# Hybrid state-space and delta-rule layer: the remaining adaLN vectors computed behind the mixers instead of beside them

## The chip, the core and the metric

One core of a Trainium2 chip runs the whole layer as one program. The metric is the device time of one execution in microseconds (us), a median over several runs. The engines have these names below: PE is TensorE (matrix products; PEld are its weight loads), DVE is VectorE, ACT is ScalarE, POOL is GpSimd, SP is the queue that issues most DMAs. Each engine works through its own instructions strictly in the order in which the program lists them; semaphores make it wait for others. SBUF is the on-chip memory, PSUM holds the results of matrix products, DRAM is the memory outside.

## The reference

512 tokens of width 2048 pass through one layer, in float32:

```python
mod = (silu(c) @ w_ada + b_ada)                       # 6 vectors of 2048: adaLN
sh_m, sc_m, g_m, sh_f, sc_f, g_f = split(mod, 6)
h = layer_norm(x) * (1 + sc_m) + sh_m
u, q, k, v, z, beta, a, gate_s, gate_g = split(h @ w_in)
y_s = s5_mixer(u, ...) @ w_up_ssm                     # state-space mixer, 64 groups
y_g = gated_deltanet(q, k, v, z, beta, a, ...) @ w_up_gdn   # delta rule, 8 heads, 8 chunks of 64 tokens
m = sigmoid(gate_s) * y_s + sigmoid(gate_g) * y_g
x = layer_norm(alpha * x + g_m * (m @ w_mix_out), ln1)
h = layer_norm(x) * (1 + sc_f) + sh_f
x = layer_norm(alpha * x + g_f * swiglu(h), ln2)
```

The two vectors `sh_m` and `sc_m` are needed before anything else. The other four (`g_m`, `sh_f`, `sc_f`, `g_f`) are a product of one row of 2048 with a 2048 x 8192 part of `w_ada`, 67.1 MB of float32, and they are what the change moves. `g_m` is first needed in the output projection `m @ w_mix_out`, `sh_f` and `sc_f` in the layer norm behind it, `g_f` in the feed-forward part.

## The kernel before

**The main line** is a sequence of large matrix products. Every weight block (128 x 1024 values) is loaded by SP into `raw`, cast by ACT to `whi` (the part that fits float32r) and subtracted by DVE into `wlo` (the rest); a product is then three PE passes, two with `whi` and one with `wlo`. There are three buffers each of `raw`, `whi` and `wlo`; a block is split two blocks ahead of its use and loaded three ahead of its split. A block feeds 24 PE passes of 512 columns, but 12 in the output projection, where only 256 of the tokens are in work at a time.

**The stages** are, in order: the start (layer norm, `sh_m`, `sc_m`, the first input columns); the mixer stage, where the products for q, k, v and z of eight delta-rule heads and seven gate pairs form the main line; the remaining gates; the gated unit (GLU) and the two up projections; the output projection in two halves of 256 tokens, each with four quarters of 512 columns; the feed-forward groups; the last layer norm.

**Side lines** are woven into the main line. A side line is a Python generator: `s5_line` (eight batches of the state-space mixer, one after the other, most of it on POOL), `gdn_prep_line` and `gdn_solve_line` (the delta-rule heads), `ln_half` (the two halves of the layer norm behind the output projection), and `ada_rest` (the four remaining adaLN vectors). The class `Order` keeps rough prices of all instructions and, after every three PE passes (`o.tick()`), emits the next piece of those side lines whose inputs it takes to be there. So the order on every engine is settled when the program is built. `o.until(...)` and `o.drain(line)` emit side lines' pieces with no main-line product between them until a condition holds; `o.drain(lnl)` stands behind the output projection and forces all that is left of the first `ln_half` there.

**One adaLN unit** is 512 columns of one vector, and there are 16 units, one after the other. `ada_line` loads 16 slices of 128 x 512 (`w`, 256 KB each, four buffers, on SP's queue) and adds them up, each times a column of `silu(c)`, into `aacc`. While the mixers' memory is in use (the list `P2` is empty) all 16 slices are DVE instructions, and a slice is emitted only when `Order` takes DVE to be nearly idle. Once the mixers' memory has been given back (`P2` is filled by `switch()`), every third slice from the second on (5 of 16) is scaled by ACT instead and added by POOL into a second sum `aacc2`, one DVE addition joins the sums, and DVE's state is no longer asked. Then PE sums over partitions: for `g_m` and `g_f` by one product with a constant (`ada_row_line`, four DVE instructions ahead of it put in the bias; ACT copies the row out and SP stores it to DRAM), for `sh_f` and `sc_f` by four small products (`ada_cols_line`).

In the kernel before, `ada_rest` is added to the side lines when the delta rule's convolution weights are ready, ahead of the first head, so all its units are emitted in the mixer stage. Helpers record every instruction, so the profile's L170 is any instruction of DVE, ACT, POOL or SP, L211 any matrix product and L216 any transpose; tiles tell them apart: `pm` and `px_fo` are the main line's products, `px_gd`, `g_...`, `St`, `vn` and `TTfull` the delta rule's, `px_s` and `s_...`, `s5...` the state-space mixer's, `px_ada` and `aacc` adaLN's.

Of the kernel before, what the change touches and what calls it, by code (L numbers as in the profile page):

```python
# [16 lines left out]
PSUM = bass.MemoryType.PSUM  # L17
DRAM = bass.MemoryType.DRAM
M, A, S = ALU.mult, ALU.add, ALU.subtract
# [17 lines left out]
def shape_constants():  # L37
    """128-wide masks, then masks of 64 x 64 diagonal blocks, stacked twice over the partitions."""
    i = np.arange(128)[:, None]
    j = np.arange(128)[None, :]  # L40
    m = [np.eye(128), j < i, i <= j, i // 16 == j // 16]
    i, j = i % 64, np.arange(64)[None, :]
    pair = (i // 2 == j // 2)
    m += [i == j, -1.0 * (pair & (j < i)), -1.0 * (pair & (i < j))]
    m += [(i // b == j // b + 1) & (i // b % 2 == 1) for b in (2, 4, 8, 16, 32)]
    return np.concatenate([a.astype(np.float32) for a in m], axis=1)
# [10 lines left out]
class Order:  # L57
    """Emission order of all engines: a main line of matrix products with side lines woven in.

    A rough model of the engines tells when each result is there, so that a side line's next piece is emitted  # L60
    about when its inputs are.
    """
    LAT = 0.12
# [12 lines left out]
    def _first(self, ap):  # L76
        """When the slot of a tile that is written for the first time gets free."""
        t = ap.tensor
        nm = ap.name
        if nm in self.ready or not hasattr(t, "tag_meta") or t.tag_meta is None:  # L80
            return 0.0
        q = self.slots.setdefault(t.tag, [])
        q.append(nm)
        n = t.tag_meta.bufs
        return self.last.get(q[-n - 1], 0.0) + self.LAT if len(q) > n else 0.0
# [73 lines left out]
class Engine:  # L159
    """An engine's instructions, with their rough price told to the order."""  # L160

# [110 lines left out]
def s5_setup(k, p, lam_re, lam_im, log_dt):  # L272
    """Powers of the discretised poles and their B factors, in [(re|im, state), group] and [(group parity, state), pair]."""
    nc, v, act, pool, pe = k.nc, k.v, k.act, k.pool, k.pe
# [98 lines left out]
def s5_batch(k, j, prm, d_col):  # L373
    """One tile of 128 channels (8 groups): u^T comes from k.du, 2 * gelu(y)^T goes to k.dz."""
    v, act, pool, pe, ld = k.v, k.act, k.pool, k.pe, k.ld
    b_re, b_im, c_re, c_im = prm
    s, t = k.s5, k.t5
# [106 lines left out]
    for ri in range(2):  # L484
        for rj in range(2):
# [3 lines left out]
            x = St[:, :, ri, 1:8, 0:7]  # L489
# [38 lines left out]
def gdn_setup(k, p, psb, a_log, dt_bias, conv_w, norm_w):  # L528
    """psb rows 0..7: beta logits, rows 8..15: decay logits, over tokens."""
    v, act, pool, pe, ld = k.v, k.act, k.pool, k.pe, k.ld  # L530
# [76 lines left out]
def gdn_conv(k, h, which, ps):  # L607
    """Causal convolution over tokens, out of PSUM."""
    s = k.gd
    a = k.tg("qkv"[which])  # L610
    col = lambda w: s.cw[:, 24 * w + 8 * which + h:24 * w + 8 * which + h + 1]
    k.act.activation(a, ps, AF.Identity, scale=col(3))
    for w in (2, 1, 0):
        d = 3 - w
        k.v.scalar_tensor_tensor(out=a[:, d:512], in0=ps[:, 0:512 - d], scalar=col(w), in1=a[:, d:512], op0=M, op1=A)
    return a
# [21 lines left out]
def gdn_prep(k, h):  # L638
    """All of a head that does not wait for the chunks before: decays, norms, the strictly lower matrix, q k^T."""
    v, act, pool, pe = k.v, k.act, k.pool, k.pe  # L640
    s, t = k.gd, k.tg
    r = Ctx()
# [104 lines left out]
def gdn_solve(k, h, r):  # L747
    """The inverse of the unit lower matrix by doubling blocks, then the chunks' recurrence and the head's output."""
    v, act, pool, pe = k.v, k.act, k.pool, k.pe
# [136 lines left out]
class Weights:  # L886
    """The stream of weight blocks, loaded and split into two float32r parts ahead of their use."""

# [63 lines left out]
    def poll(self):  # L952
        """The next block's load, once its slot is free."""
        i = self.loaded
        if i < len(self.specs) and i < self.cut + NB:
            o = self.k.o
            if i < NB or o.last.get(self.names[i - NB], 0.0) <= o.clock:
                self.load(i + 1)
# [3 lines left out]
def kernel(ctx, tc, x, c, w_ada, b_ada, w_in, lam_re, lam_im, log_dt, b_re, b_im, c_re, c_im,  # L962
# [39 lines left out]

# [1 line left out]
    ws = Weights(k, wpool)  # L1004
# [47 lines left out]

# [1 line left out]
    cst = cpool.tile([128, 128], F32, name="cst")  # L1054
# [18 lines left out]
    def by_pos(a):  # L1073
        """A tile whose tokens are ordered by their position in the chunk first, read in the tokens' order."""
        return a.rearrange("p (s c) -> p c s", s=8)

# [1 line left out]
    def split(hi, lo, src, eng=None):  # L1078
# [8 lines left out]
    def after(first):  # L1087
        """Between products: the next block's split and the side lines."""
        if first:
            ws.run_ahead()  # L1090
        o.tick()
# [11 lines left out]
    def gemm2(kt, acts, done, pre=None):  # L1103
        """Two neighbouring 128-column tiles, K in blocks of 8 slices."""
        pss = [psum_mm(), psum_mm()]
# [17 lines left out]
    def ada_line(p, col0):  # L1123
        """Per-partition partial sums of 512 adaLN columns."""
        acc = p.tile([128, 512], F32, name="aacc", tag="aacc", bufs=1)
# [34 lines left out]
    def ada_cols_line(p, j, q, dst, plus):  # L1160
        """512 columns of adaLN vector j, as columns."""
        acc = yield from ada_line(p, 2048 * j + 512 * q)
# [6 lines left out]
    def ada_row_line(p, j, q):  # L1169
        """Half of 512 columns of adaLN vector j, to a row in DRAM."""  # L1170
        acc = yield from ada_line(p, 2048 * j + 512 * q)
# [10 lines left out]

# [1 line left out]
    hT = []  # L1184
# [158 lines left out]

# [1 line left out]
    adp = ctx.enter_context(pool_of(name="adp", bufs=1, side="right"))  # L1345
# [15 lines left out]

# [1 line left out]
    gps, sps = ExitStack(), ExitStack()  # L1363
# [32 lines left out]
    o.until(lambda: k.cw_ready)  # L1396
    o.add(ada_rest())
    gate_next = iter(range(0, 32, 2))
# [7 lines left out]
    for h in range(8):  # L1406
# [9 lines left out]
        k.heads[h, 3] = z  # L1416
# [1 line left out]
    def switch():  # L1418
        """The mixers' memory becomes the operands' of the later products."""
        o.drain(s5l)  # L1420
# [22 lines left out]
        k.ada_deep = True  # L1443
        o.add(operands())

    def bt(dtype=F32R):
# [17 lines left out]

# [1 line left out]
    k.ada_deep = False  # L1466
# [62 lines left out]
    def row_of(src, q):  # L1529
        """A quarter of a row of 2048, on all partitions."""  # L1530
        return row_to(P2[1].tile([128, 512], F32, name="grow", tag="grow", bufs=1), src, q)
# [4 lines left out]

# [1 line left out]
    xa = [[None] * 4 for _ in range(4)]  # L1538
    h2 = [[None] * 16 for _ in range(2)]

    def ln_stats(st):
        """Mean, rstd and -mean * rstd of a token tile, as columns."""
        mv = cpool.tile([128, 2], F32, name="mv", tag="mv", bufs=4)
# [13 lines left out]
    def affine(r, st, g, b, how):  # L1557
        """((r - mean) * rstd) * g + b, in place; how: 0 on DVE, 1 shared, 2 without DVE."""
        if how == 0:
# [7 lines left out]
    def ln_half(hf, new_big):  # L1567
        """LN1, then LN0 with the FFN's adaLN, for 256 tokens; alpha * x1 stays in xa, h2^T goes to h2[hf]."""
        rows = []
# [84 lines left out]

# [1 line left out]

    def ffn_tile(gsj, hs):
        """2 * silu(gate) * up of one hidden tile, for the token halves hs."""
        pss = []
# [25 lines left out]
    def scaled(t, q, ps, gf):  # L1685
        """Adds the second gate's row times a product to a tile of the residual."""
        tmp = t2("ld")
        v.tensor_tensor(out=tmp, in0=ps, in1=gf, op=M)
        pool.tensor_tensor(out=xa[t][q], in0=xa[t][q], in1=tmp, op=A)
# [31 lines left out]

# [1 line left out]
    k.gf_rows += [row_to(bt(F32), drow[5], q) for q in range(2, 4)]  # L1723
# [71 lines left out]
```

## Time and profile before

| what | value |
|---|---|
| median of 3 runs | 3234.25 us (3231.43 to 3240.14) |
| span of the profiled execution | 3234.4 us |
| PE busy over the span | 3093.7 us, 96% |
| DVE, ACT, POOL busy | 49%, 29%, 27% |
| granted PE clock, mean | 0.973 |

The profile gives no time of its own for that execution beyond the span, which is 0.15 us from the median. The page divides the span into 40 slices of 81 us; the shares of the whole span hide that DVE and POOL are well used in the first third and little afterwards. The prediction therefore reads the windows by stage. "Idle" of an engine is a stretch in which it has nothing running; the granted clock is the share of PE's full rate in a stretch.

### The profile page before, as it was taken

To read this page: it belongs to the slowest core of one execution; us is meant where nothing else is said; L and a number is where in the kernel's file an instruction comes from. 1 tells how busy PE (TensorE), PEld (TensorE's weight loads), DVE (VectorE), ACT (ScalarE), POOL (GpSimd) and SP (SyncE) were. 2 spreads that over 40 slices of the span, in tenths; PEclk is the share of its full clock that TensorE was granted. 3 is DMA by queue.
4 is the path that set the end of the run, shared out by engine and by line. 5 is a ranking of instruction groups with operands and counts; after the bars stand their busy time and mean duration, and the time that the engine had idled before them with its cause. 6 is when DMAs were issued, how large, how long until landed. Compare 5 with 4: busy or idle time off the path is not lost.

```text
span 3234.4 us, 47422 instructions
## 1 busy us (share of the span) xinstructions
PE 3093.7 (96%) x19409; PEld 2699.8 (83%) x19409; DVE 1596.2 (49%) x2023; ACT 923.6 (29%) x1306; POOL 871.3 (27%) x1125
## 2 busy tenths in 40 slices
PE   6899999988999999999999999999999999999997
PEld 3587777877777788888879999998998999899895
DVE  6546776756866432444677543333233333333327
ACT  3233332222232232322354532221221222222121
POOL 4747766656754100000031102002001100200202
PEclk8899999988999999999999999999999999999998
DMA  9655556545555244445767543333333333333333
GB/s 342 213 147 156 151 162 181 151 138 169 162 143 175 79 156 134 152 147 163 237 209 202 160 150 105 92 95 108 92 92 105 98 92 98 104 93 95 108 98 117
DMA packets 521754, 458.60 MB, mean 142 GB/s; under 512 B 56144, under 2 KB 403632, under 8 KB 521536
## 3 DMA queue, kind: packets, MB, share of 16 engines
q1 hardware_dynamic: 514336, 442.47, 44.9%
q10 hardware_dynamic: 7200, 13.10, 1.1%
q8 instruction: 152, 2.49, 0.3%
q14 instruction: 66, 0.54, 0.1%
HBM read 435.60 MB, written 19.89 MB: 141 GB/s over the span
## 4 chain that ended last, share of the span: by engine, by line
PE 69%; POOL 9%; issue 5%; DVE 5%; DMA 2%; ACT 2%; SPq 1%; POOLq 0%; DVEq 0%; ACTq 0%
PE pm L211 51%; PE px_fo L211 14%; POOL s_S L170 3%; POOL s5w L170 2%; PE px_gd L211 2%; DVE aacc L170 1%; PE px_s L211 1%; SPq L170 1%; DMA w<-in_w_ada_dram 1%; DVE wlo L170 1%; DVE at L170 1%; ACT whi L170 1%; POOL g_E L170 1%; POOL g_ET L170 1%; POOL s_H L170 0%
## 5 line engine op out<-in xcount | busy, mean ns | idle before, releaser
L170 DVE TENSOR_TENSOR wlo<-raw,whi 128x1024 fp32r<-128x1024 f32 x541 | 684.0, 1266 | 899.8 <-ACT whi L170 896.8
L211 PE MATMUL pm<-at,whi 128*128 128x512 f32 (+1 forms) x3200 | 986.2, 379 | 6.4 <-ACT whi L170 3.6
L211 PE MATMUL pm<-bt,whi 128*128 128x256 f32 (+1 forms) x5312 | 988.5, 291 | 0.3 <-ACT whi L170 0.3
L170 ACT CAST whi<-raw 128x1024 fp32r<-128x1024 f32 x541 | 566.1, 1048 | 1098.6 <-PE pm L211 538.9
L211 PEld LDWEIGHTS pm<-bt,whi 128*128 128x128 f32 x5312 | 800.9, 192 | 15.9 <-ACT whi L170 0.5
L211 PEld LDWEIGHTS pm<-at,whi 128*128 128x128 f32 x3200 | 591.2, 192 | 102.9 <-ACT whi L170 4.0
L211 PE MATMUL pm<-bt,wlo 128*128 128x256 f32 (+1 forms) x2656 | 632.1, 291 | 1.5 <-DVE wlo L170 1.5
L211 PE MATMUL pm<-at,wlo 128*128 128x512 f32 (+1 forms) x1600 | 594.9, 372 | 2.5 <-DVE wlo L170 2.5
L211 PEld LDWEIGHTS pm<-bt,wlo 128*128 128x128 f32 x2656 | 447.5, 192 | 9.5 <-DVE wlo L170 1.9
L170 POOL TENSOR_TENSOR at<-at,ld 128x512 f32<-128x512 f32 x80 | 120.5, 1537 | 1148.7 <-DVE ld L170 1148.7
L211 PEld LDWEIGHTS pm<-at,wlo 128*128 128x128 f32 x1600 | 306.5, 192 | 55.9 <-DVE wlo L170 3.3
L211 PE MATMUL px_fo<-whi,at 128*128 128x512 f32 x976 | 304.7, 389 | 1.7 <-ACT whi L170 1.7
L170 DVE SCALAR_TENSOR_TENSOR aacc<-w,ccol,aacc 128x512 f32<-128x512 f32 x240 | 217.5, 906 | 26.6 <-DMA w<-in_w_ada_dram 22.4
L211 PEld LDWEIGHTS px_fo<-whi,at 128*128 128x128 f32 x976 | 183.2, 188 | 39.9 <-ACT whi L170 2.1
L211 PE MATMUL px_fo<-wlo,at 128*128 128x512 f32 x488 | 190.0, 389 | 0.8 <-DVE wlo L170 0.8
L170 POOL TENSOR_TENSOR rs<-rs,mhalf 128x1 f32<-128x1 f32 (+1 forms) x13 | 11.4, 873 | 627.8 <-DVE rs L170 627.8
L170 POOL TENSOR_TENSOR s_S<-s_S,s5w 128x64 f32<-128x64 f32 (+1 forms) x224 | 106.9, 477 | 17.6
L211 PEld LDWEIGHTS px_fo<-wlo,at 128*128 128x128 f32 x488 | 91.7, 188 | 19.9 <-DVE wlo L170 1.1
L211 PE MATMUL pm<-whi,bt 128*128 128x512 f32 x320 | 103.2, 396 | 3.3 <-DVE at L170 3.3
L211 PE MATMUL px_fo<-whi,bt 128*128 128x512 f32 x320 | 101.8, 389 | 0.0
L170 DVE SCALAR_TENSOR_TENSOR gs<-gg,pm 128x512 f32<-128x512 f32 x36 | 24.7, 687 | 154.4 <-ACT gg L170 154.4
L170 DVE TENSOR_TENSOR gs<-gs,pm 128x512 f32<-128x512 f32 x36 | 24.7, 687 | 132.5 <-PE pm L211 132.5
(374 smaller groups left out, 3139.1 us busy)
## 6 DMA issues: line engine op xcount, KB each, us to landing
raw<-in_ffn_w_in_dram SPq DMA_DIRECT2D x208, 512.0 KB, 4.1
raw<-in_w_in_dram SPq DMA_DIRECT2D x146, 512.0 KB, 3.8
w<-in_w_ada_dram SPq DMA_DIRECT2D x256, 256.0 KB, 3.6
raw<-in_ffn_w_out_dram SPq DMA_DIRECT2D x88, 512.0 KB, 3.6
wad<-in_w_ada_dram SPq DMA_DIRECT2D x64, 512.0 KB, 5.6
raw<-in_w_mix_out_dram SPq DMA_DIRECT2D x64, 512.0 KB, 4.4
raw<-in_w_up_gdn_dram SPq DMA_DIRECT2D x16, 512.0 KB, 3.4
raw<-in_w_up_ssm_dram SPq DMA_DIRECT2D x16, 512.0 KB, 3.4
```

The lines of the kernel that those rows point to most:

```text
L170: r = f(*a, **kw)
L211: r = self.e.matmul(out, **kw)
```

## The change

One line is taken out ahead of the head loop and one is put in at the end of `switch()`, the function that runs once both mixers are through. (The full diff also drops comments and docstrings, which make no instruction, and leaves blank lines in their place so that line numbers stay.)

```diff
@@ -1394,7 +1394,6 @@
     o.add(gdn_prep_line(k))
     gl = o.add(gdn_solve_line(k))
     o.until(lambda: k.cw_ready)
-    o.add(ada_rest())
     gate_next = iter(range(0, 32, 2))
...
@@ -1442,6 +1441,7 @@
                     r = nxt
         k.ada_deep = True
         o.add(operands())
+        o.add(ada_rest())
```

Since `P2` is filled by then, every unit now takes the form with ACT and POOL. Until the GLU begins (`k.ada_deep`) six loads instead of four may be ahead.

The order on DVE at the second delta-rule head, ahead of the decay table `g_E` and the state-space mixer's kernel table `s5Kc` (`cb`, `cv`, `cw` and `gt` are columns of factors, `cmix` is masks). Before:

```order
L170 TENSOR_SCALAR aacc<-w_2258,ccol 128x512
L170 TENSOR_TENSOR g_kb<-g_kt,cw 128x512
L170 SCALAR_TENSOR_TENSOR aacc<-w_2260,ccol,aacc 128x512
L170 SCALAR_TENSOR_TENSOR g_E<-px_gd,cb,g_E 128x128 x4
L170 TENSOR_TENSOR g_kt<-g_kt,gt 128x512
L170 SCALAR_TENSOR_TENSOR cv<-rk,bcol 128x4
L170 TENSOR_TENSOR wlo<-raw,whi 128x1024
L170 SCALAR_TENSOR_TENSOR aacc<-w_2262,ccol,aacc 128x512
L170 SCALAR_TENSOR_TENSOR aacc<-w_2264,ccol,aacc 128x512
L170 TENSOR_TENSOR px_s_2375<-px_s_2375,cmix 128x512
```

and with the change:

```order
L170 TENSOR_TENSOR g_kb<-g_kt,cw 128x512
L170 SCALAR_TENSOR_TENSOR g_E<-px_gd,cb,g_E 128x128 x4
L170 TENSOR_TENSOR g_kt<-g_kt,gt 128x512
L170 SCALAR_TENSOR_TENSOR cv<-rk,bcol 128x4
L170 TENSOR_TENSOR wlo<-raw,whi 128x1024
L170 TENSOR_TENSOR px_s_2323<-px_s_2323,cmix 128x512
```

The mixers' instructions stand closer together; the `aacc` slices between them are gone, here and in all of the mixer stage.

The order on DVE in the second half of the output projection with the change, where the first layer norm's affine step (`at<-at,mv,gg`, `at<-at,rs,gs`) and statistics (`st`) run (`pm<-pm,grow` multiplies a product by `g_m`):

```order
L170 TENSOR_TENSOR wlo<-raw,whi 128x1024
L170 SCALAR_TENSOR_TENSOR aacc<-w_12982,ccol,aacc 128x512
L170 SCALAR_TENSOR_TENSOR aacc<-w_13001,ccol,aacc 128x512
L170 TENSOR_TENSOR wlo<-raw,whi 128x1024
L170 SCALAR_TENSOR_TENSOR nb<-mv,rs 128x1
L170 SCALAR_TENSOR_TENSOR at<-at,mv,gg 128x512
L170 SCALAR_TENSOR_TENSOR at<-at,rs,gs 128x512
L170 TENSOR_TENSOR wlo<-raw,whi 128x1024
L170 SCALAR_TENSOR_TENSOR aacc<-w_13059,ccol,aacc 128x512
L170 TENSOR_TENSOR wlo<-raw,whi 128x1024
L170 SCALAR_TENSOR_TENSOR aacc<-w_13069,ccol,aacc 128x512
L170 TENSOR_TENSOR pm<-pm,grow 128x512
```

Before there is no `aacc` among them. Now the last five of the 16 units end behind the first `pm<-pm,grow`, among the splits of the output projection.

The order on PE at the end of the output projection (`px_tr<-cst,ld` transposes the layer norm's result, x4 being two of its 16 slices for two token tiles; `pm<-bt,whi 128x256` is the first feed-forward product; "..." leaves out main-line products). Before:

```order
L216 MATMUL px_tr<-cst,ld 128x128 x4
L211 MATMUL pm<-whi,at 128x512
L211 MATMUL pm<-wlo,at 128x512
...
L211 MATMUL pm<-wlo,bt 128x512
L211 MATMUL pm<-whi,bt 128x512
L211 MATMUL pm<-bt,whi 128x256 x2
```

and with the change:

```order
L211 MATMUL pm<-whi,bt 128x512 x2
L211 MATMUL pm<-wlo,bt 128x512
L211 MATMUL pm<-whi,bt 128x512
L216 MATMUL px_tr<-cst,ld 128x128 x16
L211 MATMUL px_ada<-aacc,half 128x512
L211 MATMUL pm<-bt,whi 128x256 x2
```

Before, all transposes of the first half stand between main-line products. Now the last sixteen of 32, and the last unit's product, stand between the output projection and the feed-forward part with nothing else for PE there.

## The prediction

> **What bounds the kernel now.** The page first: PE is busy for 96% of the span, so the question is where the other 4%, and the low clock, sit. The slices of 81 us say it:
>
> ```profile
> span 3234.4 us, 47422 instructions
> DVE  6546776756866432444677543333233333333327
> POOL 4747766656754100000031102002001100200202
> PEclk8899999988999999999999999999999999999998
> ```
>
> DVE and POOL are full in the first third and have room behind it. The windows by stage (busy us of PE, PEld, DVE, ACT and POOL; granted clock, DMA share, GB/s) put numbers to that: state-space mixer beside the delta rule (220 to 1011), delta rule alone (to 1143), gates, GLU and up projections, output projection (1500 to 1690).
>
> ```profile
> 0.00:50.00 50.00, 19.50 (x63) 9.14 (x63) 30.83 (x42) 13.73 (x21) 16.26 (x21) 0.91 0.98 346
> 220.00:1011.00 791.00, 729.98 (x4821) 604.50 (x4820) 549.88 (x804) 237.17 (x446) 532.65 (x764) 0.94 0.54 158
> 1011.00:1066.00 55.00, 52.56 (x328) 43.02 (x327) 32.83 (x53) 16.72 (x36) 12.61 (x12) 1.00 0.54 162
> 1143.00:1290.00 147.00, 147.00 (x651) 121.51 (x650) 48.07 (x46) 49.40 (x56) 0.00 (x0) 1.00 0.49 150
> 1290.00:1500.00 210.00, 210.00 (x928) 173.87 (x928) 100.51 (x112) 59.82 (x71) 0.00 (x0) 1.00 0.45 146
> 1500.00:1690.00 190.00, 183.33 (x806) 149.48 (x805) 126.56 (x153) 84.27 (x100) 24.23 (x17) 0.99 0.66 219
> 1690.00:1810.00 120.00, 113.21 (x880) 110.16 (x879) 81.58 (x117) 68.43 (x106) 31.17 (x20) 0.97 0.63 181
> ```
>
> In the 791 us of the mixer stage PE idles for 791.0 - 730.0 = 61.0 us, and a clock of 0.94 costs another 0.06 x 791 = 47.5 us: 108.5 us are lost. From 1143 to 1500 nothing is. Whom PE waited for in those 61 us (total, times, longest):
>
> ```profile
> PE px_s L211 <- POOL s_H L170: 14.4, 3, 8.6
> PE px_gd L211 <- DVE g_T L170: 9.6, 3, 4.6
> PE px_gd L211 <- DVE g_X L170: 7.8, 4, 3.8
> PE px_ada L211 <- DVE aacc L170: 6.2, 4, 5.1
> PE px_gd L211 <- POOL g_T L170: 5.1, 1, 5.1
> ```
>
> So POOL and DVE are late, by a few us at a time; `aacc` itself is named only once. The window 1011 to 1066 says the same: adaLN runs there too, the state-space mixer doesn't, and the loss is 2.4 us. What binds is POOL's state chain together with what stands in its way.
>
> **What the change removes there.** adaLN's own share of that stage, and its chain of waits:
>
> ```profile
> 220.00:1011.00 791.00, 16.25 (x78) 11.07 (x78) 225.62 (x268) 4.00 (x7) 0.94 0.54 158
> by line: issue 14.7%; PE pm L211 13.7%; POOL s_S L170 11.6%; POOL s5w L170 9.9%; DVE aacc L170 5.3%; PE px_s L211 5.2%; PE px_gd L211 4.2%; SPq L170 3.8%; DMA w<-in_w_ada_dram 3.5%; POOL g_E L170 2.0%; POOL g_ET L170 2.0%; DVE wlo L170 1.9%
> ```
>
> adaLN is 225.6 of DVE's 549.9 us, 41%, and 16.25 us of PE. On the chain `aacc` and its loads are 5.3 + 3.5 = 8.8%, or 70 us. The second way is POOL. Its timeline in the state steps, and DVE's beside it:
>
> ```profile
> 322.31 0.36 POOL L170 TENSOR_TENSOR s_S<-s_S,s5w 128x64 f32<-128x64 f32 x1
> 323.17 1.42 POOL L170 TENSOR_TENSOR s_S<-s_S,s5w 128x64 f32<-128x64 f32 x1
> 325.08 0.83 POOL L170 TENSOR_TENSOR s_S<-s_S,s5w 128x64 f32<-128x64 f32 x1
> 323.13 1.23 DVE L170 TENSOR_TENSOR wlo<-raw,whi 128x1024 fp32r<-128x1024 f32 x1 [3.33 <-ACT whi L170]
> 324.93 1.53 DVE L170 SCALAR_TENSOR_TENSOR aacc<-w,ccol,aacc 128x512 f32<-128x512 f32 x2
> ```
>
> The same step takes 0.36 us alone, 1.42 beside a split and 0.83 beside `aacc`. The 448 small steps, as groups, with each tile's shortest (min/median/max) behind them:
>
> ```profile
> L170 POOL TENSOR_TENSOR s_S<-s_S,s5w 128x64 f32<-128x64 f32 x112 | 62.8, 561 | 8.8
> L170 POOL TENSOR_TENSOR s_S<-s_S,s5w 128x8 f32<-128x8 f32 x112 | 44.1, 393 | 8.8
> L170 POOL TENSOR_TENSOR s5w<-s_S,R 128x64 f32<-128x64 f32 x56 | 26.8, 479 | 75.9 <-ACT s_S L170 72.4
> L170 POOL TENSOR_TENSOR s5w<-s_S,R8s 128x64 f32<-128x64 f32 x56 | 26.8, 479 | 4.4
> L170 POOL TENSOR_TENSOR s5w<-s_S,R64s 128x8 f32<-128x8 f32 x56 | 20.7, 370 | 4.4
> L170 POOL TENSOR_TENSOR s5w<-s_S,R 128x8 f32<-128x8 f32 x56 | 20.7, 369 | 3.8
> L170 POOL TENSOR_TENSOR s_S<-s_S,s5w x224: 214/367/1421, 225.7 to 971.9; 128x64 f32<-128x64 f32 x56, 128x8 f32<-128x8 f32 x56
> L170 POOL TENSOR_TENSOR s5w<-s_S,R8s x56: 328/354/1227, 226.2 to 953.1; 128x64 f32<-128x64 f32 x56
> ```
>
> Together 201.9 us. Undisturbed they would take 112 x 0.36 + 112 x 0.33 + 224 x 0.214 = 125 us, so 77 us are waiting for DVE; 41% of it, 32 us, is adaLN's by its share. On the chain the two groups are 21.5% or 170 us, and 170 x 77/202 x 0.41 = 27 us of that is adaLN's. So up to 70 + 27 = 97 us of the chain can go.
>
> Not all of it is gained. Two things are only put off: adaLN's 16.25 us of PE, and main-line products that used to run while the state-space mixer did. Counted in the two orders, 2,463 products stood ahead of its last store, and now 2,408; 55 fewer. A product's price is that of the undisturbed stretch in the chain:
>
> ```profile
> 1144.18 453.11 PE pm L211 x1998
> ```
>
> 453.11 / 1998 = 0.227 us, so 12.5 us. That leaves 97 - 28.7 = 68 us if nothing takes the place of what goes. Something will: the remaining 59% of DVE still makes POOL wait, and reads of DRAM (`s5B`, `g_G`) don't get faster by themselves. I take off a fifth: **55 us gained**. Bounds: below, POOL alone counts and only gets its 32 us, of which 28.7 is needed for the closer order: 3 us. Above, all of the 108.5.
>
> **What it adds behind the mixers.** The units end, by the count of products, between 3,041 and 5,288, so they begin shortly before 2,900 and last about 2,400 x 0.227 = 545 us, up to the end of the output projection. Prices:
>
> ```profile
> L170 DVE SCALAR_TENSOR_TENSOR aacc<-w,ccol,aacc x240: 735/752/2826, 228.2 to 1066.0; 128x512 f32<-128x512 f32 x120
> L170 DVE SCALAR_TENSOR_TENSOR aacc<-cst,bacol,aacc x32: 343/348/507, 290.9 to 1067.6; 128x128 f32<-128x128 f32 x32
> L170 POOL TENSOR_TENSOR at<-at,ld 128x512 f32<-128x512 f32 x80 | 120.5, 1537 | 1148.7 <-DVE ld L170 1148.7
> L170 ACT ACTIVATE f<-px_tr,mod_f 128x256 f32<-128x256 f32 x12 | 6.7, 561 | 4.1 <-PE px_tr L216 4.1
> L170 ACT ACTIVATE ld<-at,nb,rs 128x512 f32<-128x512 f32 x8 | 6.2, 810 | 2.7 <-DVE nb L170 2.7
> L170 ACT CAST bt<-f 128x256 fp32r<-128x256 f32 x12 | 4.9, 407 | 0.4
> ```
>
> A unit is 11 DVE slices and one addition, at most 12 x 0.752 = 9.0 us, and 1.4 more for a row; ACT 5 x 0.81; POOL 4 x 1.54 = 6.1; 4.19 MB of loads.
>
> *Up to 1500* eleven units come: 4 x 10.4 + 7 x 9.0 = 105 us of DVE on top of 148.6 in 357 us, 71%. Loads add 11 x 4.19 MB / 357 us = 129 GB/s; at the start's rate (0.98 of the DMA engines for 346 GB/s) that is 0.37 on top of 0.45 to 0.49. A block lasts 24 x 0.227 = 5.4 us and is split two ahead. Hidden: 2 us.
>
> *In the output projection* five units come, one of columns and four of rows: 9.0 + 41.6 = 51 us of DVE on top of 126.6 in 190, 93%, and the second half, with the layer norm, is fuller than the first. A block lasts 12 x 0.227 = 2.7 us there, and two blocks less ACT's 1.05 and DVE's 1.25 us leave 3.1 us of slack for a split. The loads, 21 MB or 110 GB/s, raise the DMA share from 0.66 to 0.97. The lower end is 0; the upper all 51 us, and 31 us for 20 POOL additions that DVE may have to wait for. I take 18, nearer to the free room (63 us) than to the price.
>
> *At its end* sixteen transposes, eight slices, now stand where PE has nothing else. ACT needs 8 x (0.56 + 0.41) + 4 x 0.81 = 11 us for them; 0 if they are through by then, 11 plus the last unit's row if not; 9 taken. Then PE idles 27 us more, and the clock costs, as from 1690 to 1810 (3.6 us beside 6.8 idle) or from 1500 to 1690 (1.9 beside 6.7), a fifth to a half: 7.
>
> The sum: 3234.4 - 55 + 2 + 18 + 9 + 7 = 3215.4, against a profiled span that stands 0.15 us from the median. **Forecast: 3215 us.**
>
> The Trainium skill ("SBUF — State Buffer", section "SBUF: two separate sides") says that POOL and a DVE instruction with two SBUF inputs take a shared port pair by an exclusive lock for a whole instruction. The 1.42 and 0.83 us agree. By that rule the 64 late POOL additions turn the same lock against DVE: 20 of them beside the output projection hold it for 31 us, and the sum, were all of it on PE, would be 3246.
>
> **The rivals.**
>
> *DVE overfull beside the output projection (slower).* Place: the splits of `w_mix_out` behind `aacc` slices that wait for loads at a DMA share of 0.97, or behind POOL's additions. It decides once `wlo` comes over 3.1 us late, block after block. Then the 51 us are not hidden, the tail is 11, and the clock takes a fifth, 13: 3234.4 - 55 + 75 = 3254. For it: 93%, and the second half of the stage idles already. Against it: 63 us are free there. Page and rule: the lock just cited would work in this direction.
>
> *POOL alone (no change).* The state chain keeps its pace, PE waits as before but earlier in the program; 15 gained, 13 lost: 3232. For it: POOL heads the list of PE's waits, and the loss is small where only adaLN and the delta rule run. Against it: 8.8% of the chain is adaLN's own.
>
> *All hidden (faster by more).* The full 68 us, with 8 lost: 3174. For it: no loss from 1143 to 1500 at present. Against it: the tail in PE's order.
>
> That the units don't move is excluded by the order, which has none ahead of 2,880 products.
>
> **How the numbers follow.** Forecast 0.45, overfull 0.21, POOL alone 0.17, all hidden 0.17. About 0.3%, 9.7 us, is what a measurement can tell from no change: 3224.5 to 3244. The forecast's own spread (3195 to 3230) leaves 0.03 of its 0.45 in that band, and all of POOL alone's 0.17 lies in it: faster 0.42 + 0.17 = 0.59, same 0.20, slower 0.21. The range 3168 to 3256 takes in the middles of all four cases; about half of the overfull case and half of the hidden one, 0.19 together, lie outside.
>
> **What would show it.** In the mixer stage: idle of PE down from 61 to some 25 us, clock above 0.96, small `s_S` steps of 64 below 0.5 us on average; right for the lock if the mean falls, wrong if the stage shortens and it doesn't. In the output projection: `pm` waiting for `wlo` by 10 to 25 us; transposes in a run with PE idle ahead of the feed-forward part. A gain of under 30 us in the mixer stage, or a loss of over 50 behind it, would make the prediction wrong.

## The result, and the profile after

The changed kernel takes 3279.81 us (median of 4 runs, 3277.46 to 3288.4), the kernel before on the same chip 3236.34 us (4 runs, 3231.43 to 3240.14): ratio 1.0146, 95% interval 1.0125 to 1.0168. It is **slower by 43 us**, where 20 us of gain were forecast, and outside the range of 3168 to 3256. The profiled execution is 41.6 us longer than before's. From its page, rows that were shown for before:

```profile
span 3276.0 us, 47553 instructions
DVE  6644554444434667775767543323333323333337
PEclk9899999999999999999888999999999999999998
```

DVE is emptier early and fuller in the middle, as was meant; but three slices of PE's clock, 20 to 22 (1556 to 1802 us), now show 8. Counting main-line products and reading when each one ends in the two traces says where the time went:

| product that ends | place | before, us | after, us | difference | of it in this part |
|---|---|---|---|---|---|
| 2,880 | mixers are through | 1126.9 | 1058.8 | -68.1 | -68.1 |
| 4,512 | start of the output projection | 1498.1 | 1447.2 | -50.9 | +17.2 |
| 5,287 | its end | 1686.9 | 1706.2 | +19.3 | +70.2 |
| 6,060 | first feed-forward products | 1791.1 | 1833.3 | +42.2 | +22.9 |
| last | end | 3234.4 | 3276.0 | +41.6 | -0.6 |

So the mixers gain 68 us, and 110 us are lost behind them, 70 of these in the output projection. The windows of the changed kernel (columns as before: PE, PEld, DVE, ACT, POOL, granted clock, DMA share, GB/s): the state-space mixer beside the delta rule, the stretch from the end of the mixers to the output projection in two, the output projection, and what follows it:

```profile
220.00:928.00 708.00, 670.37 (x4556) 556.51 (x4555) 334.75 (x519) 232.09 (x437) 476.50 (x764) 0.98 0.32 84
1066.00:1219.00 153.00, 153.00 (x670) 125.02 (x669) 102.80 (x116) 68.84 (x93) 30.03 (x18) 1.00 0.82 271
1219.00:1447.00 228.00, 223.78 (x993) 184.27 (x992) 165.38 (x192) 81.58 (x104) 40.75 (x26) 0.99 0.76 248
1447.00:1707.00 260.00, 213.84 (x811) 162.83 (x810) 175.61 (x215) 87.17 (x101) 44.84 (x29) 0.89 0.70 230
1707.00:1833.00 126.00, 108.73 (x811) 103.33 (x810) 88.81 (x128) 70.61 (x108) 35.69 (x24) 0.91 0.66 193
```

In the mixer stage PE's idle time fell from 61.0 to 708.0 - 670.4 = 37.6 us and the clock rose from 0.94 to 0.98. In the output projection (260 us) PE idles 46.2 us and the clock of 0.89 costs another 0.11 x 260 = 28.6; and yet nothing else is full: DVE is busy for 68%, POOL for 17%, and the DMA engines for 70%, hardly more than the 66% of before. adaLN's own part of the output projection (its PE time is 10.89 us ahead of it, from 1066 on, and 2.05 behind it, up to 1833):

```profile
1447.00:1707.00 260.00, 5.92 (x22) 3.43 (x22) 53.55 (x67) 4.96 (x8) 27.75 (x17) 0.89 0.70 230
```

DVE got 53.6 us of adaLN beside the output projection, as forecast (51). So the work is as heavy as I took it to be, and the engine that does it has room. What is late is the weights. ACT's first step on a block is the cast `whi<-raw`; whom it waited for in the output projection (total, times, longest us), before and after:

```profile
ACT whi L170 <- PE pm L211: 45.3, 27, 4.4
ACT whi L170 <- DMA raw<-in_w_mix_out_dram: 35.6, 19, 4.9
```

```profile
ACT whi L170 <- DMA raw<-in_w_mix_out_dram: 110.6, 35, 10.2
```

Before, ACT waited more for PE than for blocks; now it waits mostly for the block's load (for PE 36.1 us). And SP, which issues all loads in one order, waited for these, before:

```profile
SPq L170 <- DVE wlo L170: 109.5, 55, 6.2
```

and after:

```profile
SPq L170 <- POOL aacc L170: 46.9, 11, 9.6
SPq L170 <- DVE aacc L170: 44.7, 26, 8.0
...
SPq L170 <- ACT aacc L170: 7.3, 6, 2.1
```

SP's waits on adaLN's instructions are new: 46.9 + 44.7 + 7.3 = 99 us, nearly all of it ahead of loads of slices. SP stands at the load of a slice `w`, whose buffer (one of four) is free only when DVE or POOL has added an earlier slice; the load of the next weight block stands behind it. A piece of the chain of waits of the changed kernel (start us, us, what) shows one lap:

```profile
1486.15 4.58 DMA raw<-in_w_mix_out_dram
...
1490.84 1.06 ACT whi L170
...
1491.95 1.11 issue
1493.06 1.80 DVE aacc L170
1494.88 0.33 SPq L170
...
1495.26 6.33 DMA raw<-in_w_mix_out_dram
```

And the timelines of SP, DVE, ACT and POOL there (start us, us; x2 are two in a row; in brackets the idle time before):

```profile
1486.15 0.43 SPq L170 DMA_DIRECT2D raw<-in_w_mix_out_dram  x1
1487.57 0.33 SPq L170 DMA_DIRECT2D w<-in_w_ada_dram  x1
1488.00 0.38 SPq L170 DMA_DIRECT2D raw<-in_w_mix_out_dram  x1
1494.33 0.88 SPq L170 DMA_DIRECT2D w<-in_w_ada_dram  x2
1495.26 9.13 SPq L170 DMA_DIRECT2D raw<-in_w_mix_out_dram  x4
...
1507.65 0.38 SPq L170 DMA_DIRECT2D raw<-in_w_mix_out_dram  x1
```

```profile
1491.92 1.23 DVE L170 TENSOR_TENSOR wlo<-raw,whi 128x1024 fp32r<-128x1024 f32 x1 [4.38 <-ACT whi L170]
1493.06 1.79 DVE L170 SCALAR_TENSOR_TENSOR aacc<-w,ccol,aacc 128x512 f32<-128x512 f32 x1
```

```profile
1491.79 0.72 ACT L170 ACTIVATE w<-w,ccol 128x512 f32<-128x512 f32 x1
```

```profile
1492.59 1.71 POOL L170 TENSOR_TENSOR aacc<-aacc,w 128x512 f32<-128x512 f32 x1 [9.19 <-ACT w L170]
```

**It is a loop.** DVE stands idle for 4.38 us because a block is not there; then comes the block's split `wlo` (the chain's 1.11 us of "issue"), then, behind it on DVE, a slice `aacc`; that slice's end frees a buffer; SP issues `w` and, right behind it, the next `raw`, which lands 6.3 us later. The same lap has a second way round, over ACT and POOL: ACT scales its slice only behind the block's cast, POOL adds it after 9.19 us of idle time, and the end of that addition at 1494.30 frees the buffer of the first of the two `w` at 1494.33, for which SP had waited since 1488.4. It ends only 0.55 us ahead of DVE's slice, so either engine alone would have held the lap up.

From one `raw` to the next on the chain are 1495.26 - 1486.15 = 9.1 us. In this lap SP issued two blocks (at 1486.15 and 1488.00), 4.6 us for each, where PE needs 2.7; in the next one, from 1495.26 to 1507.65, four, 3.1 us for each. Over the stage it is 260 us for 62 blocks, 4.2 us each; before 189 / 62 = 3.05. Every engine waits in this loop, and so none is full.

### The profile page after: what moved, and what is told of

Same layout as the page of the kernel before. It is cut to its first block, busy times and chain, and to the rows that moved or that the text cites. A ratio compares the mean times of both kernels' runs of the same rounds, so it can differ in the third digit from the quotient of the medians.

```text
span 3276.0 us, 47553 instructions
## 1 busy us (share of the span) xinstructions
PE 3097.1 (95%) x19409; PEld 2689.2 (82%) x19409; DVE 1561.0 (48%) x1959; ACT 977.0 (30%) x1386; POOL 921.3 (28%) x1189
## 4 chain that ended last, share of the span: by engine, by line
PE 48%; DVE 3%; DMA 3%; issue 1%; ACT 1%; SPq 0%; ACTq 0%; POOL 0%; DVEq 0%
PE pm L211 34%; PE px_fo L211 14%; DMA raw<-in_w_mix_out_dram 3%; DVE aacc L170 1%; DVE at L170 1%; DVE wlo L170 1%; ACT whi L170 1%; SPq L170 0%; PE px_ada L211 0%; DVE raw L170 0%; DVE bt L170 0%; DVE pm L170 0%; DVE st L170 0%; DMA gg<-dg 0%; PE px_tr L216 0%
## 5 line engine op out<-in xcount | busy, mean ns | idle before, releaser
L170 DVE TENSOR_TENSOR wlo<-raw,whi 128x1024 fp32r<-128x1024 f32 x541 | 692.1, 1280 | 882.3 <-ACT whi L170 872.3
L211 PE MATMUL pm<-at,whi 128*128 128x512 f32 (+1 forms) x3200 | 974.9, 376 | 9.7 <-ACT whi L170 5.0
L211 PEld LDWEIGHTS pm<-bt,whi 128*128 128x128 f32 x5312 | 802.9, 192 | 17.2 <-issue 1.0
L211 PEld LDWEIGHTS pm<-at,whi 128*128 128x128 f32 x3200 | 584.6, 190 | 105.2 <-ACT whi L170 5.4
L170 POOL TENSOR_TENSOR aacc<-aacc,w 128x512 f32<-128x512 f32 x58 | 93.9, 1618 | 459.5 <-ACT w L170 459.3
L170 DVE SCALAR_TENSOR_TENSOR aacc<-w,ccol,aacc 128x512 f32<-128x512 f32 x143 | 142.5, 997 | 9.8 <-DMA w<-in_w_ada_dram 8.0
L211 PE MATMUL pm<-whi,bt 128*128 128x512 f32 x320 | 114.2, 428 | 19.9 <-DVE at L170 18.3
L211 PEld LDWEIGHTS pm<-whi,bt 128*128 128x128 f32 x320 | 65.2, 204 | 39.0 <-DVE at L170 21.2
L211 PE MATMUL pm<-whi,at 128*128 128x512 f32 x224 | 79.3, 425 | 15.0 <-ACT whi L170 15.0
```

Source lines behind the costliest of these rows:

```text
L170: r = f(*a, **kw)
L211: r = self.e.matmul(out, **kw)
```

## The experiments

The theory from the traces is the **queue**: the output projection is slow since SP's order makes the weight blocks wait for adaLN's buffers. Its rivals are **work** (DVE's time, or POOL's additions with their port, delay the splits) and **bytes** (71 loads of 256 KB, some 19 MB, share the DMA engines). A useful measure is the time between the ends of products 2,880 and 6,060, which holds all that the change loses: 664.2 us before, 774.5 after. The table is for reading along; the rows and what follows come below. Its times behind the median are those of each kernel's profiled execution.

| kernel | median us | product 2,880 ends | 2,880 to 6,060 | output projection |
|---|---|---|---|---|
| before | 3231 to 3236 | 1126.9 | 664.2 | 188.8 |
| the change | 3279.8 | 1058.8 | 774.5 | 259.0 |
| 1 slice of 16 | 3186.7 | 1067.1 | 674.1 | 185.7 |
| loads alone | 3197.3 | 1065.0 | 683.0 | 198.3 |
| work without loads | 3216.7 | 1066.5 | 704.1 | 213.3 |
| 8 buffers | 3220.5 | 1068.7 | 700.9 | 214.4 |
| no ACT, no POOL | 3280.8 | 1064.8 | 766.4 | 261.9 |
| loads by POOL | 3247.5 | 1069.3 | 732.9 | 215.0 |
| `g_f` held back | 3231.3 | 1076.0 | 695.9 | 206.1 |
| from the state-space mixer's end | 3207.4 | 1068.5 | 694.2 | 204.6 |
| the same with 8 buffers | 3194.9 | 1073.3 | 673.5 | 188.2 |

**One slice of sixteen.** What is the place worth when hardly anything is put there?

```diff
-        for kt in range(16):
-            while len(raws) < min(16, kt + depth):
+        for kt in range(1):
+            while len(raws) < min(1, kt + depth):
...
```

> The changed kernel, with 1 of the 16 slices of every adaLN unit loaded and added; the other 15 are left out, with the additions into the second sum, so the last four vectors are not the reference's. What is left of a unit is its product, its bias and its row. All theories: the mixer stage keeps the 69 us it gained, and whatever of the loss behind it comes from adaLN's slices is gone. If the whole loss behind the mixers (about 110 us, of which some 88 from the first output projection product to the first full feed-forward tile) is the slices' doing, 3236 - 69 + 0 to 10 = 3167 to 3177 us. If the closer order itself, without slices, delayed the later stages, over 3195 us.

Measured: 3186.65 us (ratio 0.9860, 0.9842 to 0.9877), between the two forecasts. The output projection takes what it took before, with the clock back at full:

```profile
1452.00:1638.00 186.00, 180.80 (x802) 147.63 (x801) 126.97 (x154) 82.33 (x97) 24.39 (x16) 1.00 0.64 217
```

So the slices and their loads make 774.5 - 674.1 = 100 of the 110 us; the place in the program and the reductions on PE cost 674.1 - 664.2 = 10.

**More buffers.** Eight buffers in turn for the slices, and as many loads ahead as in the change, so that the buffer of a load is free well before SP comes to it. The same work and the same bytes:

```diff
-            if not k.ada_deep or n % 6 < 4:
+            if n % 8 < 4:
                 raw = p.tile([128, 512], F32, name="w1", tag="w1", bufs=4)
             else:
-                raw = P2[1].tile([128, 512], F32, name="gg", tag="gg", bufs=2)
+                raw = P2[1].tile([128, 512], F32, name="w1", tag="w2", bufs=4)
```

> The changed kernel with eight buffers for adaLN's slices instead of four (four more from the memory that the mixers gave back), with the same four loads ahead. Queue theory: SP stands still on loads of slices whose buffer is not yet read (106 us of waits for aacc in the 260 us of the output projection), and the weight loads queued behind them come late; with twice the buffers those waits and most of the loss go: 3195 to 3235 us, SP's waits for aacc there under 25 us. Overfull DVE or POOL's lock: the same instructions run on the same engines, so the loss stays: 3265 to 3285 us. DMA bandwidth: the same bytes, and no faster: 3265 or more.

Measured: 3220.49 us (0.9961, 0.9948 to 0.9973): 59 us less than the change, and faster than before. Its window of the output projection and what was left of SP's waits there:

```profile
1453.00:1667.00 214.00, 190.40 (x801) 148.82 (x801) 171.85 (x212) 92.18 (x110) 46.16 (x31) 0.98 0.74 260
```

```profile
SPq L170 <- ACT aacc L170: 8.5, 2, 6.5
...
SPq L170 <- DVE aacc L170: 4.8, 6, 1.5
```

99 us of waits on adaLN became 13, of which the 8.5 are the stores of two finished rows and no load of a slice; and nearly the same DVE work (172 us, now 80% of a shorter window) passes. With the run on POOL's queue below this is the main evidence for the queue. The units also end earlier, the last at product 5,039 and not 5,288, which is a consequence of the buffers and shortens the tail too; so 53 loads instead of 71 fall into the output projection.

**No ACT and no POOL.** All sixteen slices on DVE, as in the mixer stage before. If POOL's additions were what is in the way, this would help:

```diff
-            if acc2 is not None and kt % 3 == 1:
+            if False:
...
```

> The changed kernel with all 16 slices of a unit on DVE, as they were beside the mixers: no ACT scaling, no POOL addition. Lock theory (POOL's additions hold DVE up): better, 3240 to 3260 us. Overfull DVE: five more slices of 0.75 us a unit, so worse, 3290 to 3310 us. Queue theory: a buffer is free as soon as one engine has read it instead of two in turn, so the 54 us that SP waited for POOL go and some of them come back as waits for DVE: 3245 to 3270 us.

Measured: 3280.79 us (1.0151, 1.0128 to 1.0173), no better than the change; all three expectations missed, the queue's too (3245 to 3270). The wait on the buffers only changed its name (SP's wait, then the window):

```profile
SPq L170 <- DVE aacc L170: 97.7, 50, 8.8
```

```profile
1445.00:1707.00 262.00, 209.17 (x815) 158.39 (x815) 183.71 (x240) 78.03 (x88) 20.43 (x14) 0.92 0.71 235
```

97.7 us on DVE's slices stand for the 99 on POOL's, DVE's and ACT's, in a stage as long as the change's and with DVE again busy for only 70% (183.7 of 262). POOL's additions, and the port that they share with DVE, are not the cause of the late loss; who adds the slices makes no difference as long as SP waits for it.

**Loads alone, and work alone.** First the sixteen loads with one slice added; then all the work, with one load that serves sixteen times:

```diff
             yield raws[kt]
+            if kt:
+                continue
...
```

```diff
-            k.sync.dma_start(out=raw, in_=w_ada[0, k0:k0 + 128, col0:col0 + 512])
+            if k0 == 0:
+                k.sync.dma_start(out=raw, in_=w_ada[0, k0:k0 + 128, col0:col0 + 512])
...
-                v.scalar_tensor_tensor(out=acc, in0=raws[kt], scalar=sc, in1=acc, op0=M, op1=A)
+                v.scalar_tensor_tensor(out=acc, in0=raws[0], scalar=sc, in1=acc, op0=M, op1=A)
...
```

> The changed kernel with all 256 loads of slices kept, but 15 of 16 slices of every unit never scaled or added (left out of the result). A buffer is then free as soon as its load has landed. Queue theory: SP has nothing to wait for, so the loss behind the mixers is that of the bytes alone: 3190 to 3205 us, between the 3187 of one slice and the 3220 of eight buffers, and SP's waits for aacc in the output projection vanish. DMA bandwidth: the bytes are all there, so most of the 93 us between one slice and all stays: 3250 us or more.

> The changed kernel with one load a unit, whose slice is then used 16 times (so 15 of 16 slices are left out of the result), and with all of the work of DVE, ACT and POOL, at about the old pace (four units end within the output projection instead of five). Queue theory: without loads on SP nothing stands ahead of the weight loads: 3195 to 3215 us. Overfull DVE or POOL's lock: the work is all there: 3255 to 3280 us.

Measured: 3197.3 us (0.9897, 0.9867 to 0.9928) for the loads, 3216.66 (0.9951, 0.9933 to 0.9969) for the work; the first is where the queue theory put it, the second 2 us above its range. The output projection in each:

```profile
1447.00:1646.00 199.00, 188.00 (x805) 150.42 (x804) 130.38 (x164) 80.04 (x91) 23.97 (x16) 0.98 0.75 255
```

```profile
1453.00:1666.00 213.00, 192.21 (x807) 151.54 (x806) 181.39 (x221) 92.03 (x111) 48.53 (x32) 0.97 0.59 197
```

Over the kernel with one slice, from product 2,880 to 6,060, the loads cost 683.0 - 674.1 = 9 us and the work 704.1 - 674.1 = 30; together they would be 39, and the change has 774.5 - 674.1 = 100. **61 us are left over**, in the only one of the three in which loads have to wait for the work. They are the most that this wait can have cost, and not its price: loads that nothing holds up come earlier, and 35 of them fall into the output projection in the loads-alone run, 71 in the change, so its 9 us are low for the bytes. The work is there in full (46 slices added on DVE and 18 additions on POOL in that stage, 45 and 17 in the change), and it costs 30 us. With eight buffers work and bytes cost 700.9 - 674.1 = 27 together, no more than the work alone.

**The slices' loads on POOL's queue.** The queue theory again, without more buffers: POOL issues `w`, so that no weight block can stand behind one. (The first line is the price in the planner, which would have spread them otherwise.)

```diff
-                self.o.run(k, 1.0 if k == "p" else 0.06, out, ins, 0.05 + out.nbytes() / 345e3)
+                self.o.run(k, 0.06, out, ins, 0.05 + out.nbytes() / 345e3)
...
-            k.sync.dma_start(out=raw, in_=w_ada[0, k0:k0 + 128, col0:col0 + 512])
+            pool.dma_start(out=raw, in_=w_ada[0, k0:k0 + 128, col0:col0 + 512])
```

> The changed kernel with the slices' loads issued by POOL instead of SP; the order of all other instructions nearly as it was (28 instead of 16 transposes are left at the end of the output projection, some 6 us more). Queue theory: a load that waits for its buffer now holds up POOL, which has little else to do there, and no longer the weights: output projection 260 down to 200 to 225 us, in all 3215 to 3245 us. DMA bandwidth, overfull DVE, lock: 3270 us or more, since bytes and work are unchanged.

Measured: 3247.46 us (1.005, 1.0021 to 1.0078), a little above what the queue theory gave (3215 to 3245). The output projection:

```profile
1453.00:1668.00 215.00, 193.12 (x799) 152.30 (x798) 177.51 (x211) 82.86 (x91) 80.44 (x101) 0.96 0.82 277
```

POOL's waits ahead of the loads of slices there:

```profile
POOL w L170 <- DVE aacc L170: 56.7, 30, 8.4
POOL w L170 <- ACT aacc L170: 40.0, 4, 13.4
```

The waits for buffers are all still there, 56.7 + 40.0 = 97 us, but they stand on a queue that brings no weights. The output projection has as many slices and loads as in the change (46 slices added on DVE, 74 loads) and is as good as with eight buffers, at the highest DMA share of any output projection here (0.82), so the engines could have moved those bytes. It takes 29 us more than with one slice (215 against 186), which is what bytes and work cost there together; the other 45 of the change's 260 us are the queue's. The miss is behind it: 28 transposes instead of 16 stand in the tail of this order, and it takes 134 us (126 in the change, 103 with eight buffers). So the output projection's loss goes by two ways that share no edit, and what they have in common is that no weight block waits behind a slice's load. The Trainium skill ("DMA: Bandwidth & Descriptors", section "Issuing engines are not separate DMA queues") says that starting transfers from several engines saves no more than the sequencer's time for starting them. Here a second queue took 45 us off a stage (260 to 215): what it saved was the weight blocks' waiting ahead of their start.

**The last four units held back.** `g_f` isn't needed ahead of the feed-forward part; its four units wait until that begins:

```diff
+        while not k.ffn_go:
+            yield 2.0
         for q in range(4):
             yield from ada_row_line(adp, 5, q)
+            k.gf_n = q + 1
...
-            o.until(lambda: k.ada_done)
+            o.until(lambda: k.gf_n > q)
...
```

> The changed kernel with the last four units (g_f) held back until the second half of the layer norm is through, so that they run beside the first full feed-forward tiles, where DVE is 33% and the DMA engines 35% busy; each quarter of the feed-forward output then waits for its own unit only. One unit is left in the output projection instead of five. If the loss sits where units and short weight blocks (2.7 us) meet, most of it goes: 3236 - 69 + 15 for the gates to the merge + 10 to 20 = 3190 to 3205 us. If the loss is anywhere beside adaLN, it moves into the feed-forward part: 3240 to 3270 us.

Measured: 3231.26 us (1.0001, 0.9987 to 1.0015), between the two forecasts (3190 to 3205, 3240 to 3270); the profiled execution took 3240.4, the longest of ten. The output projection shrinks to 206 us and the tail to 103; part of the loss then turns up behind them:

```profile
1772.00:1895.00 123.00, 108.47 (x797) 104.26 (x796) 76.09 (x98) 56.42 (x82) 20.12 (x12) 0.92 0.72 211
```

Products 6,060 to 6,831 take 122.6 us where they took 102.0 before. A block lasts 102.0 / 32 = 3.2 us there, and SP waits 20.3 us for DVE's and 17.6 for POOL's slices: the stall goes with the units, into a stage whose blocks are short too.

**Where the mixers' gain comes from.** Two runs on the kernel before: its loads without the work (15 of 16 slices not added), and its work without 15 of 16 loads, with edits like those shown above.

> The kernel before, adaLN beside the mixers, with all 256 loads kept and 15 of 16 slices never added on DVE (left out of the result). It splits the gain of the mixer stage. If DVE's 226 us of slices were in the way (its queue, and POOL's small steps that wait beside them): the stage is as short as with the change, 3170 to 3190 us, and a small step of 128x64 takes 0.43 to 0.45 us on average instead of 0.56. If the loads were in the way (SP's queue, DVE waiting for slices): the stage keeps its length, 3220 us or more.

> The kernel before with all of adaLN's slice work at its old place beside the mixers, but 15 of the 16 loads of each unit left out (the first slice is used sixteen times, so the vectors are wrong). The order of the units is close to before: they end between products 660 and 2,891, not 660 and 2,650. It is the other half of the run of before with the loads alone, whose mixer stage took 869 to 874 us, against 907 before, 849 with neither work nor loads. Work theory (what adaLN costs in the mixer stage is DVE's slices and what they do to POOL): product 2,880 comes at 1,110 us or later (the stage from 220 takes 885 to 905), small state steps of 64 above 0.52 us on average, time 3215 to 3232. Loads theory (the costs are the waits for slices and SP's queue): product 2,880 at 1,075 to 1,100 (stage 855 to 880), small steps below 0.50 us, time 3190 to 3212.

Measured: 3198.4 us (0.9901, 0.9862 to 0.9939) without the work, between the two forecasts and nearer to the work theory's, and 3245.15 (1.004, 1.0011 to 1.0069) without the loads, above what either theory gave, though its product 2,880 and its small steps come out on the work theory's side. Product 2,880 ends at 1089.2 and at 1136.6 us (1126.9 before, 1058.8 in the change). POOL's groups of small state steps of 64 (busy us, mean ns | idle) in the change, in the loads alone and in the work alone:

```profile
L170 POOL TENSOR_TENSOR s_S<-s_S,s5w 128x64 f32<-128x64 f32 x112 | 48.6, 434 | 8.8
```

```profile
L170 POOL TENSOR_TENSOR s_S<-s_S,s5w 128x64 f32<-128x64 f32 x112 | 52.1, 465 | 8.8
```

```profile
L170 POOL TENSOR_TENSOR s_S<-s_S,s5w 128x64 f32<-128x64 f32 x112 | 58.7, 524 | 8.8
```

Taking the loads away while the work stays gains nothing in the mixers; taking the work away gains 38 us, and the loads and the reductions with it 30 more. So the work on DVE is what the mixers paid for first, and POOL's steps move with it (561 ns before). The 10 us by which the work alone is worse than before, in an order that ends its units at product 2,891 instead of 2,650, are not explained.

**A version that beats both.** The line goes back to its old place, but its first unit waits for the end of the state-space mixer, so that the units end between products 2,496 and 4,757: ahead of most of the output projection.

```diff
     def ada_rest():
+        while not s5l.done:
+            yield 2.0
```

> The line back at its old place, but the first unit waits until the state-space mixer is through (by the count of products from about 2,410 on instead of 2,880), four buffers. Five units run beside the rest of the delta rule and the first gates, where POOL is free and PE lost nothing; one or two instead of five are left in the output projection. Queue theory: the mixer stage keeps most of its 69 us (60), the gates to the merge lose 15, the projection 15 instead of 88: 3195 to 3215 us. If any unit beside the mixers costs the gain: 3230 us or more.

> The same with eight buffers for slices once the mixers' memory is free. Queue theory: the remaining waits of SP for aacc go, and units end earlier: 3185 to 3205 us, at least as fast as with four. Bandwidth or work: as with four buffers.

Measured: 3207.38 us (0.9916, 0.9894 to 0.9938), and with eight buffers once the mixers' memory is free 3194.86 us (**0.9873, 0.9847 to 0.9900**), 1.3% faster than before and 2.6% faster than the change. The output projection of the second one is through as fast as before any of this:

```profile
1457.00:1645.00 188.00, 182.99 (x796) 147.47 (x795) 137.17 (x166) 82.12 (x94) 29.49 (x19) 0.99 0.73 239
```

The mixers keep most of their gain (product 2,880 ends at 1068.5 and 1073.3 us), though some units run beside the delta rule.

## Why the prediction was wrong

To hold the sum against the trace, adaLN's 10.89 + 5.92 + 2.05 = 18.9 us of PE, which the prediction had taken off the mixers' gain as put off, are booked there again:

| term | forecast | measured |
|---|---|---|
| mixer stage | -55 | -68.1 + 18.9 = -49 |
| gates, GLU, merge | +2 | 17.2 - 10.9 = +6 |
| output projection | +18 | 70.2 - 5.9 = +64 |
| its end, with the clock | +9 + 7 | 22.9 - 2.1 = +21 |

The sum is 61 us off, and 46 of them are one term.

**The bound was right, and the gain nearly.** POOL and DVE were late in the mixers, and the gain of this execution came within 6 us. That it came so near is in part luck: seven of the runs above have the same instructions up to product 2,880 as the change and end it at 1064.8 to 1076.0 us, 1067.1 in the middle, by which the gain is 41 us and not 49; and the fifth that was taken off was a guess. The sign named for the lock came too: the mean of the small steps of 64 fell from 561 to 434 ns, below the 500 asked for, and the clock rose to 0.98; only PE's idle time fell less (to 38 us, not 25). By the work-alone and loads-alone runs the price was first of all DVE's work (38 of 68 us; 30 went with the loads and reductions). How the 97 us split into the chain's own 70 and POOL's 27 no run has tested.

**The failed step** is the term of 18 us for the output projection, measured as 64, and in it the sentence "two blocks less ACT's 1.05 and DVE's 1.25 us leave 3.1 us of slack for a split". DVE's price there was right (51 forecast, 53.6 measured), and the work by itself costs 27 us in that stage (213 against 186), not far from the 18 taken; bytes and work together cost 29 (215). But the slack of a split counts from the block's landing, and the prediction let the loads cost nothing but a share of the DMA engines, "from 0.66 to 0.97". The share became 0.70, because the loads were not issued. SP's queue, in which the loads of `w` now stand between 62 loads of weight blocks, had no term at all, and by the run on POOL's queue it is 45 us of the 260. The traces of before already held two rows that would have called for a term: SP spent 109.5 us of that stage waiting for a block's buffer, so a block was issued as soon as one came free and none was in store; and ACT already waited 35.6 us for blocks.

**Why the same waits did little harm up to 1500.** SP waited for adaLN's buffers there as well:

```profile
SPq L170 <- POOL aacc L170: 87.0, 32, 7.2
...
SPq L170 <- DVE aacc L170: 39.8, 47, 4.0
```

That is 127 us in 381, and PE was still busy for 153.0 of 153 and 223.8 of 228 us. "Hidden: 2 us" was not far off (6 measured), but for a reason that the next stage doesn't share: a block lasts 5.4 us on PE there and 2.7 in the output projection, and a loop that brings a block every 4.2 us, as it did in the output projection, keeps up with the first and not with the second. Its pace ahead of 1500 was not measured by itself.

**The tail** was named rightly and sized low: PE's waits from 1707 to 1833 us are first of all transposes waiting for ACT,

```profile
PE px_tr L216 <- ACT ld L170: 13.3, 4, 6.5
PE px_ada L211 <- DVE aacc L170: 3.1, 1, 3.1
```

16.4 us where 9 were taken, with a clock of 0.91 on top: 0.09 x 126 = 11 us.

**The rivals.** "DVE overfull" had the place, the sign and nearly the size (75 for the two last rows, measured 85), but its mechanism was the price of DVE's work, with the splits late for PE: PE waited only 10.0 us for `wlo`, and longer for ACT's casts and for DVE's `at`:

```profile
PE pm L211 <- DVE at L170: 18.3, 6, 4.8
PE pm L211 <- ACT whi L170: 16.5, 7, 5.3
PE pm L211 <- DVE wlo L170: 10.0, 15, 1.0
```

With the full work but eight buffers these waits are

```profile
PE pm L211 <- DVE wlo L170: 13.0, 11, 5.0
PE pm L211 <- DVE at L170: 8.8, 5, 2.9
PE pm L211 <- ACT whi L170: 1.8, 2, 1.0
```

What went is the wait for casts, that is for late blocks, and half of that for `at`, which stands on DVE behind splits and slices (in the lap above PE waits 2.88 us for one, at 1497.60). The wait for `wlo`, which was this rival's sign, didn't shrink; DVE was 80% busy, and the kernel faster than before. Nearest to "all hidden" (3174) comes the version that beats both, 3195, which gives the loop no place.

The Trainium skill ("SBUF — State Buffer", section "SBUF: two separate sides") was cited for a lock between POOL and DVE. If that lock made the late loss, the run without POOL's additions would have lost most of it, since DVE got only 8 us more to do in exchange (183.7 against 175.6); it was no faster (3280.8 against 3279.8). DVE's slices do take longer beside the output projection, 962 ns on average against 752 at the median of before; as an estimate from these two, the lock cost the slices at most 45 x 0.21 = 9 us there. In the mixers the small steps agree with it (561 ns before, 434 after); for the late loss it is not the cause.

**What stays open.** Which part of the 30 us of work alone is DVE's and which POOL's and ACT's; what the bytes cost by themselves when as many fall into the output projection as in the change; the 6 us up to 1500 beyond adaLN's PE time; and the 10 us of the work-alone run in the mixers.

## What to carry to other kernels

Before a load is moved into a stage, look at what its buffer waits for and at what stands behind it on the issuing queue: a load that waits for its buffer holds back all loads behind it, and if what frees the buffer stands on an engine behind the consumers of those loads, the wait closes into a loop in which every engine idles. The row to look for is the queue's own wait, together with how much time one block buys in that stage; the busy shares of the engines and of the DMA (68% and 70% here) didn't show it. Where such a move is wanted, give the moved loads enough buffers that their issue never waits, and end them before the stage with the shortest blocks.

## What was not expected of the hardware

The costs of loads and work did not add up: 9 us for the loads alone (half as many of them beside the output projection), 30 for the work, 100 for both. A DMA share of 0.82 (277 GB/s) went with an output projection of 215 us, and one of 0.70 (230 GB/s) with 260: the busier DMA engines were the faster stage. And the granted clock was low where PE stalled often: 0.89 where it idled 46 of 260 us in many short gaps, 1.00 where it idled 5 of 186. In the first, 28.6 / 46.2 = 0.6 us of clock went with each us of waiting; in other windows shown here it is 0.4 (all on DVE: 0.08 x 262 = 21 us with 52.8) to 0.7 (`g_f` held back: 0.08 x 123 = 9.8 with 14.5). The prediction had taken a fifth to a half.
